# A two-layer decoder trunk on one core: first norm's squares summed per tile on TensorE, float32 logits in four column groups, moved constants, another block order

## The chip, the core and the metric

The kernel runs on one core of one Trainium2 chip. The metric is the device time of one execution in microseconds (us). The engines are TensorE (PE, matrix products, with a separate row PEld for weight loads), VectorE (DVE), ScalarE (ACT), GpSimd (POOL) and SyncE (SP), which here only issues DMAs. Each engine works through its own list of instructions in order.

## The reference, cut to what matters

512 tokens of 1024 float32 channels pass through two layers. The two places that the change touches directly are the first norm with the small logits made from it, and the logits of the forget gate after layer 0.

```python
def rms_norm(x, w):                       # mean over the 1024 channels of a token
    return x * rsqrt(mean(x * x, -1) + 1e-6) * w

# layer 0, mixer
h = rms_norm(x, pre_mix_norm[0])
proj = h @ w_in                           # 1024 x (8 heads x (k, q, v, z) x 128, and 16 columns)
b_logit, a_in = proj[..., o2:o2 + 8], proj[..., o2 + 8:]
beta = sigmoid(b_logit)
g = -exp(a_log) * softplus(a_in + dt_bias)
# q, k, v: convolution over 4 tokens and silu; then the gated delta rule per head, in chunks
...
# after layer 0
kvf = rms_norm(x, kv_norm) @ w_kv         # 1024 x (1024 keys, 1024 values, 16 columns)
f_logit = kvf[..., 2048:] + b_forget
log_f_cum = cumsum(log_sigmoid(f_logit))
# layer 1: attention with 16 heads of 64, its scores shifted by log_f_cum; each layer ends in a SwiGLU
```

## The kernel before, in words

**Tiles.** Everything lies transposed: a tile is 128 channels by 512 tokens, so the residual x is eight tiles (`a` in the profile). A product's weights come as blocks of 1024 rows by 128 columns, 512 KB each. A block (`wf`) is split into a high half `wh` (ScalarE's copy into float32r, the rounded type that TensorE multiplies in one pass) and a low half `wl` (block minus high half, on VectorE, sometimes GpSimd). x is split likewise after the norm's gain: pairs named `b` and `h`. `product` (L699) then makes three matmuls of 128x512 for each of the eight row tiles: high by high, low by high, high by low. A block is 24 such matmuls. Blocks are read in a fixed sequence (`seq`); `land` (L611) issues their loads on SP's queue, `halve` (L620) makes the halves, `next_halves` and `halver` (L658, L669) do so ahead of use. There are four buffers of each of wf, wh, wl.

**Order.** The program is written as cooperating generators that record instructions; `Plan.cost` (L202) gives each one an assumed time, `groups_of` (L302) joins neighbouring matmuls of one kind into groups of less than 0.8 us of that assumed time, and `listed` and `ordered` (L362, L412) sort the groups into one order per engine. So a change to any cost moves instructions everywhere. All instructions are issued from one helper and carry line 102 in the trace; they are told apart by their tiles. PSUM banks are `prj` (3 of them, for products), `mid` (2), `sm` (2) and `ob` (1).

**The start (`main`, L1592).** k0's weights come in four quarters of 128x256 between x's eight tiles, on SP's queue, and the small weights (1024x16, `w_small`) behind x's seventh tile and whole blocks behind all of it. The gains and four constants come on ScalarE's queue. TensorE first does 11 products of ones. Then, for each x tile, `halves_of` (L753) makes the pair (high half with the gain on ScalarE, low half on VectorE) and `accumulate` (L724) squares it on ScalarE and adds the square to one tile on VectorE. When all eight are added, `token_sums` (L730) sums over channels with 16 small matmuls (each 32 rows of output, one column), and `token_rsqrt` (L737) makes the factor `rs` per token: VectorE, a power on GpSimd, four transposes, a copy by ScalarE. Blocks that are multiplied before `rs` is there use the unscaled pairs and are multiplied by `rs` behind the product; `scaled_halves` (L1637) makes scaled pairs for the later ones. `first_factor` (L1633) runs the factor.

**Logits.** With k0 run the 16 columns of the small weights, its high and low halves side by side as 32 columns: `thin_product` (L706) makes two float32r matmuls of 32 rows of output for each x tile, 16 in all, into one bank `prj`. `gates` (L949) takes it from there: `token_logits` (L923) multiplies by `rs`, transposes four times 32 rows by 128 tokens into `sm`, and adds the halves. The same function serves the forget gate after layer 0 (`forget`, L1394), whose 16 matmuls stand in `main` at L1724 and read the second set of the norm `n2`.

**Blocks.** `GDN_ORDER` (L1557) lists the 32 blocks of k, q, z and v (8 heads each) in the order in which `main` multiplies them; the constants' casts (`identb` and others) and the recurrences of the heads stand among them.

Of the kernel before, what the change touches and what calls it, by code (L numbers as in the profile page):

```python
# [120 lines left out]
class Plan:  # L121
# [80 lines left out]
    def cost(self, eng, op, out, ins, kw):  # L202
# [8 lines left out]
        if eng == "PE":  # L211
# [224 lines left out]
def trunk(  # L436
# [183 lines left out]
    def halve(pieces=1, act=ACT, dve=None):  # L620
# [10 lines left out]
        elif not thin:  # L631
            lo = plan.tile("wl", 4, wpool, [P, KT, P], F32R, nm("wl"))
            ready.append((hi[:, :, :cols], lo[:, :, :cols]))
        else:

            lo = hi[:, :, cols:]
            ready.append(hi[:, :, : 2 * cols])
# [3 lines left out]
        step = n // pieces  # L641

# [94 lines left out]
    def token_rsqrt(acc, tok, r, use):  # L737
# [3 lines left out]
        yield ("#sm", plan.ready(acc[:, tok]))  # L741
        ps = sm()
        token_sums(ps, acc, cs)
# [15 lines left out]
    class Norm:  # L759


        def __init__(self, name, sets):
            self.name, self.sets = name, sets
            self.h = [[alloc() for _ in range(KT)] for _, alloc in sets]
            self.acc, self.rs, self.r = w_tile(), w_tile(), small([P, NC], "tokn", 2)

        def factor(self, i, tok):
# [3 lines left out]
            yield from token_rsqrt(self.acc, tok, self.r, use)  # L771
# [96 lines left out]
    def add(w, eng, n=KT, cols=P, thin=False, ahead=False):  # L868
# [54 lines left out]
    def token_logits(ps, norm, dst, n=2):  # L923
# [8 lines left out]
        part = ps[:, 0 : NC * m].rearrange("p (c i h) -> p c i h", i=n, h=16)  # L932
        DVE.tensor_copy(dst, part[:, :, 0])
        if n == 2:
            DVE.tensor_tensor(out=dst, in0=part[:, :, 1], in1=dst, op=ALU.add)
# [617 lines left out]
    def eng_mix():  # L1553
# [4 lines left out]
        "k0 k1 k2 z0 z1 k3 k4 k5 k6 q0 z2 k7 z3 z4 z5 z6 "  # L1558
        "z7 v0 q1 v1 q2 v2 q3 v3 q4 v4 q5 v5 q6 v6 q7 v7"
    ).split()]  # L1560
    for kind, hd in GDN_ORDER:
        add(w_gdn["qkvz".index(kind) * GH + hd], DVE)
        if (kind, hd) == ("k", 0):
            add(w_small[0], DVE, cols=16, thin=True)
# [17 lines left out]
    add(w_small[1], DVE, cols=16, thin=True)  # L1582
# [9 lines left out]
    def main():  # L1592
# [9 lines left out]
        ACT.dma_start(out=cst_sb, in_=cst[:, 0:2])  # L1602
# [212 lines left out]
```

## Time and profile before

| | |
|---|---|
| three runs | 1323.44, 1323.25, 1322.71 us |
| median | 1323.25 us |
| the profiled execution | 1322.56 us |
| its span in the trace | 1320.8 us |
| TensorE busy | 1307.2 us (99%) |
| VectorE, ScalarE, GpSimd busy | 768.5, 588.6, 105.7 us |

How to read it: the span is the time between the first and the last record of the profiled execution, the execution's own time is 1.8 us longer. Matmuls overlap in the pipeline, so the time of one (0.38 us in its record) is longer than the distance to the next. The page's chain of work that ended last is 98% TensorE. The rows on which the prediction rests follow below.

### The profile page before, as it was taken

Reading aid. Unit: us, or ns where it says so; the run is one execution under the profiler, and the core shown is the slowest. Engines: PE = TensorE matmul, PEld = TensorE weight load, DVE = VectorE, ACT = ScalarE, POOL = GpSimd, SP = SyncE. Lnnn points to the kernel's source line nnn. Section 1 sums busy time; section 2 is a strip of 40 time slices with the busy share of each in tenths; the row PEclk is TensorE's granted clock in tenths of the full one; section 3 lists DMA queues with packets and bytes.
Section 4 is the critical chain, followed back from the end, with each engine's and each line's share of the span. In section 5 each row is a group of like instructions: output and inputs, shape, how many; then the busy total and the mean of one; then the engine's idle time right before and its main releaser. Section 6 shows DMA issues by size and latency. Waiting matters only on the chain.

```text
span 1320.8 us, 19699 instructions
## 1 busy us (share of the span) xinstructions
PE 1307.2 (99%) x7906; PEld 1088.2 (82%) x7906; DVE 768.5 (58%) x1362; ACT 588.6 (45%) x1119; POOL 105.7 (8%) x104
## 2 busy tenths in 40 slices
PE   8999999999999999999999999999999999999997
PEld 6788788889988888888899787777988888888886
DVE  7979877757764432244468575787775444442223
ACT  6574466647432222233345474685543222223221
POOL 0020000003200000000022310200310000000000
PEclk8999999999999999999999999999999999999999
DMA  7213220215223233323321230201222222233121
GB/s 228 74 49 112 67 74 23 65 52 173 80 96 96 93 95 98 112 98 96 105 89 65 80 99 33 97 2 47 98 91 101 96 96 96 96 98 110 65 95 64
DMA packets 36683, 115.73 MB, mean 88 GB/s; under 512 B 6336, under 2 KB 7104, under 8 KB 36592
## 3 DMA queue, kind: packets, MB, share of 16 engines
q1 hardware_dynamic: 34720, 111.95, 25.8%
q10 hardware_dynamic: 1872, 2.53, 0.6%
q8 instruction: 62, 1.02, 0.3%
q14 instruction: 29, 0.24, 0.1%
HBM read 112.30 MB, written 2.16 MB: 87 GB/s over the span
## 4 chain that ended last, share of the span: by engine, by line
PE 98%; DMA 1%; issue 1%; DVE 0%; ACT 0%; ACTq 0%; DVEq 0%; POOLq 0%; POOL 0%
PE prj L102 78%; PE mid L102 7%; PE sm L102 6%; PE ob L102 6%; DMA wf<-in_w_gdn_dram 0%; DMA a<-in_xT_dram 0%; DVE w L102 0%; ACT w L102 0%; DVE b L102 0%; ACT b L102 0%; ACT y L102 0%; DVE h L102 0%; DVE a L102 0%; ACTq L102 0%; ACT wh L102 0%
## 5 line engine op out<-in xcount | busy, mean ns | idle before, releaser
L102 PE MATMUL prj<-h,wh 128*128 128x512 f32 (+1 forms) x1840 | 584.0, 388 | 0.0
L102 PEld LDWEIGHTS prj<-h,wh 128*128 128x128 f32 x1840 | 345.7, 188 | 66.1
L102 ACT ACTIVATE wh<-wf 128x1024 fp32r<-128x1024 f32 (+2 forms) x202 | 207.6, 1031 | 429.4 <-PE prj L102 212.4
L102 PE MATMUL prj<-h,wl 128*128 128x512 f32 (+1 forms) x920 | 353.3, 384 | 0.0
L102 DVE TENSOR_TENSOR wl<-wf,wh 128x1024 fp32r<-128x1024 f32 (+2 forms) x188 | 226.3, 1205 | 160.5 <-ACT wh L102 160.0
L102 PE MATMUL prj<-b,wh 128*128 128x512 f32 (+2 forms) x992 | 289.1, 369 | 3.7 <-ACT b L102 3.5
L102 PEld LDWEIGHTS prj<-b,wh 128*128 128x128 f32 (+1 forms) x992 | 176.0, 187 | 36.5 <-ACT b L102 4.9
L102 PEld LDWEIGHTS prj<-h,wl 128*128 128x128 f32 x920 | 173.2, 188 | 31.1
L102 DVE TENSOR_TENSOR w<-prj,w 128x512 f32<-128x512 f32 (+1 forms) x88 | 60.8, 691 | 202.4 <-PE prj L102 201.7
L102 PE MATMUL prj<-b,wl 128*128 128x512 f32 (+1 forms) x480 | 172.5, 359 | 0.0
L102 PEld LDWEIGHTS prj<-b,wl 128*128 128x128 f32 x480 | 91.3, 190 | 11.1
L102 DVE TENSOR_TENSOR w<-w,w 128x512 f32<-128x512 f32 (+1 forms) x123 | 81.4, 669 | 31.9 <-ACT w L102 27.0
L102 PE MATMUL prj<-wh,b 128*128 128x512 f32 x260 | 88.1, 399 | 0.0
L102 ACT ACTIVATE b<-w 64x512 fp32r<-64x512 f32 (+1 forms) x92 | 57.0, 628 | 24.5 <-DVE w L102 23.8
L102 PEld LDWEIGHTS prj<-wh,b 128*128 128x128 f32 x260 | 48.9, 188 | 10.2 <-issue 0.7
L102 PE MATMUL prj<-wl,b 128*128 128x512 f32 x130 | 50.7, 390 | 0.0
L102 PE MATMUL prj<-h,b 128*128 128x256 f32 x288 | 46.7, 284 | 0.0
L102 POOL TENSOR_TENSOR wl<-wf,wh 128x1024 fp32r<-128x1024 f32 x12 | 29.2, 2437 | 194.1 <-ACT wh L102 192.6
L102 DVE TENSOR_TENSOR b<-w,b 128x512 fp32r<-128x512 f32 (+1 forms) x60 | 42.3, 706 | 2.7 <-ACT b L102 2.3
L102 ACT ACTIVATE b<-sm,m 128x256 f32<-128x256 f32 (+3 forms) x64 | 33.4, 524 | 20.6 <-DVE m L102 20.3
L102 PEld LDWEIGHTS prj<-h,b 128*128 128x128 f32 x288 | 39.7, 192 | 0.0
L102 ACT ACTIVATE b<-prj 128x512 f32<-128x512 f32 (+1 forms) x49 | 26.5, 540 | 29.3 <-PE prj L102 29.3
(216 smaller groups left out, 1485.2 us busy)
## 6 DMA issues: line engine op xcount, KB each, us to landing
wf<-in_w_ffn_in_dram SPq DMA_DIRECT2D x88, 512.0 KB
wf<-in_w_gdn_dram SPq DMA_DIRECT2D x31, 512.0 KB
wf<-in_w_down_dram SPq DMA_DIRECT2D x22, 512.0 KB
wf<-in_w_ffn_out_dram SPq DMA_DIRECT2D x16, 512.0 KB
wf<-in_w_gdn_out_dram SPq DMA_DIRECT2D x8, 512.0 KB
wf<-in_w_q_dram SPq DMA_DIRECT2D x8, 512.0 KB
wf<-in_w_k_dram SPq DMA_DIRECT2D x8, 512.0 KB
wf<-in_w_v_dram SPq DMA_DIRECT2D x8, 512.0 KB
```

The source lines that it names most:

```text
L102: self.call(*[real(v) for v in self.args], **{k: real(v) for k, v in self.kw.items()})
```

## The change

- **Squares.** Each x tile's squares are summed by TensorE as they are made, into an `sm` bank held for it: eight sets of 16 small matmuls that accumulate. The additions on VectorE go; VectorE makes three of the squares (tiles 1, 3, 5), ScalarE five.
- **Loads.** k0's first quarter goes ahead of x's first tile; the four constants go from ScalarE's queue to SyncE's, behind x or among the weight blocks.
- **Scaled halves.** The low halves of the scaled pairs 1, 3 and 5 are made on GpSimd.
- **Block order.** `GDN_ORDER` is another permutation.
- **Logits.** `thin_product` makes one float32 matmul for each x tile from x itself and the small weights times the gain (on VectorE; 16 columns, 16 more set to zero by GpSimd): eight, each 32 rows of output, spread over four groups of output rows by k % 4. `token_logits` multiplies and transposes all 128 rows, and one reduction adds the four parts. The planner's cost of such a matmul is new, and `main` allows a switch to other work only after every fourth.

```diff
             elif cols == 32:
-                t = 0.021
+                t = 0.021 if n == 1 else n / 2400
...
+        def thin_weights():
+            w = f(hi)[:, :, :32]
+            POOL.memset(w[:, :, cols:], 0.0)
+            g = gains_sb[:, thin * KT : (thin + 1) * KT].unsqueeze(2).broadcast_to([P, KT, cols])
+            (dve or eng).tensor_tensor(out=w[:, :, :cols], in0=t[:, :, :cols], in1=g, op=ALU.mult)
...
-    def thin_product(ps, w, k, xp):
-        for i in range(2):
-            PE.matmul(ps[0:32], lhsT=w[:, k], rhs=xp[:, i], start=k == 0 and i == 0, stop=k == KT - 1 and i == 1)
+    def thin_product(ps, w, k, x):
+        PE.matmul(ps[ck(k % 4, 32)], lhsT=w[:, k], rhs=x[k], start=k < 4, stop=k >= 4)
...
-    def token_sums(ps, src, chunks):
+    def token_sums(ps, src, chunks, first=True, last=True):
...
-                          rhs=ones[:, 0:1], start=True, stop=True)
+                          rhs=ones[:, 0:1], start=first and (last or c == 0), stop=last and (first or c == NC - 1))
...
-        m = n * 16
-        DVE.tensor_tensor(out=rows[0:m], in0=ps[0:m], in1=norm.rs[0:m], op=ALU.mult)
+        DVE.tensor_tensor(out=rows, in0=ps, in1=norm.rs, op=ALU.mult)
...
-            PE.transpose(ps[:, ck(c, m)], rows[0:m, ck(c)], ident[0:m, 0:m])
...
+            PE.transpose(ps[:, ck(c)], rows[:, ck(c)], ident)
+        DVE.tensor_reduce(
+            out=dst, in_=ps.rearrange("p (c i h) -> p c h i", i=4, h=32)[:, :, 0:16], axis=AX.X, op=ALU.add)
...
-        "k0 k1 k2 z0 z1 k3 k4 k5 k6 q0 z2 k7 z3 z4 z5 z6 "
+        "k0 k1 z0 k2 k3 k4 k5 k6 z1 k7 q0 z2 z3 z4 z5 v0 "
...
-        ACT.dma_start(out=cst_sb, in_=cst[:, 0:2])
...
+        SP.dma_start(out=cst_sb, in_=cst[:, 0:2])
...
             if k > 1:
-                accumulate(n0.acc, x0[k - 2], k - 2, full, ACT, DVE)
+                sq = w_tile()
+                if k - 2 in (1,3,5):
+                    DVE.tensor_tensor(out=sq, in0=x0[k - 2], in1=x0[k - 2], op=ALU.mult)
+                else:
+                    ACT.activation(sq, x0[k - 2], AF.Square)
+                squares.append(sq)
...
+            for k in range(KT):
+                yield (plan.ready(squares[k]),)
+                token_sums(sums, squares[k], range(NC), k == 0, k == KT - 1)
...
-                    DVE.tensor_tensor(out=hs[k - 1][:, 1], in0=t[k - 1], in1=f(hs[k - 1][:, 0]), op=ALU.subtract)
+                    (POOL if k - 1 in (1, 3, 5) else DVE).tensor_tensor(
+                        out=hs[k - 1][:, 1], in0=t[k - 1], in1=f(hs[k - 1][:, 0]), op=ALU.subtract)
...
-                    thin_product(pb, ws[1], k, h[k])
+                    thin_product(pb, ws[1], k, x0)
...
         for k in range(KT):
-            thin_product(ps, w, k, n2.h[1][k])
-            yield ()
+            thin_product(ps, w, k, x)
+            if k % 4 == 3:
+                yield ()
```

TensorE's order at the start, before, from the product with x's fourth tile on. `prj_152` is k0's bank, `prj_193` the logits' bank, `b_` the pairs of x, `sm_214` the sums, `mid_251` the transposed factor.

```order
L102 MATMUL prj_152<-b_183,wh_131 128x512
L102 MATMUL prj_152<-b_183,wl_140 128x512
L102 MATMUL prj_152<-b_183,wh_131 128x512
L102 MATMUL sm_214<-ones,w_117 32x1 x16
L102 MATMUL prj_193<-b_183,wh_181 32x512 x2
L102 MATMUL prj_193<-b_189,wh_181 32x512 x2
L102 MATMUL prj_193<-b_200,wh_181 32x512 x2
L102 MATMUL prj_193<-b_205,wh_181 32x512 x2
L102 MATMUL mid_251<-cst_sb,tokn_244 128x128 x4
L102 MATMUL prj_193<-b_211,wh_181 32x512 x2
```

One set of sums stood there, and five pairs of logit matmuls in a near row. The same place after, with `prj_137` as k0's bank, `prj_185` the logits', `a_` x itself, `sm_157` the sums:

```order
L102 MATMUL prj_185<-a_97,wh_114 32x512
L102 MATMUL prj_185<-a_104,wh_114 32x512
L102 MATMUL prj_185<-a_110,wh_114 32x512
L102 MATMUL sm_157<-ones,w_182 32x1 x16
L102 MATMUL prj_137<-b_175,wh_119 128x512
L102 MATMUL prj_137<-b_175,wl_123 128x512
L102 MATMUL prj_137<-b_175,wh_119 128x512
L102 MATMUL sm_157<-ones,w_213 32x1 x16
L102 MATMUL prj_185<-a_117,wh_114 32x512
L102 MATMUL prj_137<-b_189,wh_119 128x512
L102 MATMUL prj_137<-b_189,wl_123 128x512
L102 MATMUL prj_137<-b_189,wh_119 128x512
```

Three logit matmuls stand in a row, and from the fourth on each stands alone between k0's matmuls or the sums. SyncE's queue of DMAs at the start, before:

```order
L102 DMA a_83<-in_xT_dram 128x512
L102 DMA a_97<-in_xT_dram 128x512
L102 DMA a_104<-in_xT_dram 128x512
L102 DMA wf_109<-in_w_gdn_dram 128x256
L102 DMA a_113<-in_xT_dram 128x512
L102 DMA a_119<-in_xT_dram 128x512
L102 DMA wf_109<-in_w_gdn_dram 128x256
L102 DMA a_124<-in_xT_dram 128x512
L102 DMA a_129<-in_xT_dram 128x512
L102 DMA wf_134<-in_w_small_dram 128x8x16
```

Seven x tiles and two of k0's quarters stood ahead of the small weights. After:

```order
L102 DMA wf_87<-in_w_gdn_dram 128x256
L102 DMA a_97<-in_xT_dram 128x512
L102 DMA a_104<-in_xT_dram 128x512
L102 DMA wf_87<-in_w_gdn_dram 128x256
L102 DMA a_110<-in_xT_dram 128x512
L102 DMA wf_87<-in_w_gdn_dram 128x256
L102 DMA a_117<-in_xT_dram 128x512
L102 DMA wf_121<-in_w_small_dram 128x8x16
L102 DMA wf_87<-in_w_gdn_dram 128x256
L102 DMA a_128<-in_xT_dram 128x512
L102 DMA a_133<-in_xT_dram 128x512
L102 DMA a_141<-in_xT_dram 128x512
```

Four x tiles and three quarters stand ahead of the small weights, and a quarter stands first. TensorE's order at the forget gate's logits, before, with the last matmul of the block ahead of them:

```order
L102 MATMUL prj_6944<-h_6566,wh_6826 128x512
L102 MATMUL prj_6991<-b_6424,wh_6854 32x512 x2
L102 MATMUL prj_6991<-b_6474,wh_6854 32x512 x2
L102 MATMUL prj_6991<-b_6485,wh_6854 32x512 x2
L102 MATMUL prj_6991<-b_6516,wh_6854 32x512 x2
```

and after, where x's tiles (`a_`) are read:

```order
L102 MATMUL prj_7043<-h_6665,wh_6925 128x512
L102 MATMUL prj_7090<-a_3521,wh_6953 32x512
L102 MATMUL prj_7090<-a_3528,wh_6953 32x512
L102 MATMUL prj_7090<-a_3535,wh_6953 32x512
L102 MATMUL prj_7090<-a_3541,wh_6953 32x512
L102 MATMUL prj_7090<-a_3546,wh_6953 32x512
```

Sixteen matmuls became eight, in a row in both orders, of which the fences show the first.

## Rows read from the trace of the kernel before

**Rows 1.** The page: span, TensorE's busy time, instructions
```profile
span 1320.8 us, 19699 instructions
...
PE 1307.2 (99%) x7906; PEld 1088.2 (82%) x7906; DVE 768.5 (58%) x1362; ACT 588.6 (45%) x1119; POOL 105.7 (8%) x104
```

**Rows 2.** Stretches of 2 us: length, busy time (instructions) by engine, clock, DMA, GB/s
```profile
6.00:8.00 2.00, 0.00 (x0) 0.00 (x0) 0.72 (x2) 1.38 (x3) 0.00 (x0) 1.00 1.04 386
8.00:10.00 2.00, 1.60 (x3) 0.72 (x3) 1.90 (x4) 2.00 (x6) 0.00 (x0) 0.59 1.02 256
10.00:12.00 2.00, 1.22 (x2) 0.50 (x2) 2.00 (x5) 2.00 (x6) 0.00 (x0) 0.50 0.95 269
...
14.00:16.00 2.00, 2.00 (x8) 0.94 (x7) 2.00 (x4) 2.00 (x5) 0.00 (x0) 0.70 0.95 334
```

**Rows 3.** Order of time on TensorE, 8 to 24 us: start, time, instruction, tiles, count
```profile
8.22 0.67 PE L102 MATMUL prj<-b,wh 128*128 128x512 f32 x1 [2.59 <-ACT b L102]
...
16.36 0.40 PE L102 MATMUL prj<-b,wh 128*128 128x512 f32 x1
16.68 0.43 PE L102 MATMUL sm<-ones,w 128*32 128x1 f32 x32
17.05 2.03 PE L102 MATMUL prj<-b,wh 128*32 128x512 f32 x8
...
21.37 0.43 PE L102 MATMUL sm<-cst_sb,w 32*128 32x32 f32 x4
21.73 0.50 PE L102 MATMUL prj<-b,wh 128*128 128x512 f32 x1
...
23.00 0.62 PE L102 MATMUL prj<-b,wh 128*128 128x512 f32 x2
...
23.68 0.62 PE L102 MATMUL prj<-b,wh 128*128 128x512 f32 x2
```

**Rows 4.** Order of time, all engines, 0 to 14 us: first x, small weights, halves
```profile
3.75 1.39 ACT L102 ACTIVATE w<-a 128x512 f32<-128x512 f32 x2 [1.52 <-DMA a<-in_xT_dram]
...
6.98 0.64 SPq L102 DMA_DIRECT2D wf<-in_w_small_dram  x1
7.15 0.40 ACT L102 ACTIVATE wh<-wf 128x256 fp32r<-128x256 f32 x1
...
7.46 0.71 ACT L102 ACTIVATE b<-a,gains_sb 128x512 fp32r<-128x512 f32 x1
...
11.68 0.29 ACT L102 ACTIVATE wh<-wf 128x128 fp32r<-128x128 f32 x1
```

**Rows 5.** Order of time on TensorE in attention: matmuls of 64 output rows
```profile
781.60 1.09 PE L102 MATMUL ob<-b,h 128*64 128x128 f32 x16
...
791.95 0.88 PE L102 MATMUL ob<-b,h 128*64 128x128 f32 x12
```

**Rows 6.** Order of time on TensorE: the second norm's logits
```profile
735.60 4.11 PE L102 MATMUL prj<-b,wh 128*32 128x512 f32 x17
739.54 0.40 PE L102 MATMUL prj<-b,wl 128*128 128x512 f32 x1
```

**Rows 7.** Later stretches, columns as in rows 2
```profile
20.00:60.00 40.00, 40.00 (x181) 31.46 (x180) 37.74 (x69) 21.42 (x36) 0.00 (x0) 1.00 0.37 119
...
340.00:680.00 340.00, 340.00 (x1602) 284.00 (x1601) 150.08 (x186) 106.64 (x143) 6.51 (x4) 1.00 0.32 103
```

**Rows 8.** Order of time on TensorE at the end of the recurrences
```profile
289.00 0.49 PE L102 MATMUL sm<-rhs,b 128*128 128x128 f32 x2 [0.64 <-DVE rhs L102]
```

**Rows 9.** GpSimd's weight halves as a group, then the order of time near 703
```profile
L102 POOL TENSOR_TENSOR wl<-wf,wh 128x1024 fp32r<-128x1024 f32 x12 | 29.2, 2437 | 194.1 <-ACT wh L102 192.6 <-issue 1.5
...
702.81 1.76 DVE L102 SCALAR_TENSOR_TENSOR h<-a,gains_sb,h 128x256 fp32r<-128x256 f32 x2
703.37 0.92 POOL L102 TENSOR_TENSOR a<-b,a 128x256 f32<-128x256 f32 x1
...
705.23 0.47 DVE L102 SCALAR_TENSOR_TENSOR h<-a,gains_sb,h 128x256 fp32r<-128x256 f32 x1
```

More of the change, by code (lines that the diff above doesn't have):

```diff
@@ L630, in halve @@
             ready.append((hi, lo))
-        elif not thin:
+        elif thin is None:
             lo = plan.tile("wl", 4, wpool, [P, KT, P], F32R, nm("wl"))
@@ L641, in halve @@
         step = n // pieces
+        def thin_weights():
[3 more added lines that the diff above has]
+            (dve or eng).tensor_tensor(out=w[:, :, :cols], in0=t[:, :, :cols], in1=g, op=ALU.mult)
+        if thin is not None:
+            return [thin_weights]
         def piece(k):
@@ L734, in token_sums, with token_rsqrt @@
                 PE.matmul(ps[ck(b, 32), c : c + 1], lhsT=src[:, c * P + b * 32 : c * P + b * 32 + 32],
-                          rhs=ones[:, 0:1], start=True, stop=True)
-    def token_rsqrt(acc, tok, r, use):
+                          rhs=ones[:, 0:1], start=first and (last or c == 0), stop=last and (first or c == NC - 1))
+    def token_rsqrt(acc, tok, r, use, ps=None):
         cs = range(tok.start // P, tok.stop // P)
         sl = slice(cs[0], cs[-1] + 1)
-        yield ("#sm", plan.ready(acc[:, tok]))
-        ps = sm()
-        token_sums(ps, acc, cs)
+        if ps is None:
+            yield ("#sm", plan.ready(acc[:, tok]))
+            ps = sm()
+            token_sums(ps, acc, cs)
+        else:
+            yield (plan.ready(ps[:, sl]),)
         m = small([P, NC], "tokr", 4)
@@ L759, in trunk, with __init__ @@
     class Norm:
-        def __init__(self, name, sets):
+        def __init__(self, name, sets, sums=None):
             self.name, self.sets = name, sets
             self.h = [[alloc() for _ in range(KT)] for _, alloc in sets]
-            self.acc, self.rs, self.r = w_tile(), w_tile(), small([P, NC], "tokn", 2)
+            self.sums = sums
+            self.acc, self.rs, self.r = None if sums is not None else w_tile(), w_tile(), small([P, NC], "tokn", 2)
         def factor(self, i, tok):
@@ L769, in use @@
                 ACT.activation(self.rs[:, tok], ps, AF.Copy)
-            yield from token_rsqrt(self.acc, tok, self.r, use)
+            yield from token_rsqrt(self.acc, tok, self.r, use, self.sums)
             signal(f"{self.name}.rs{i}")
@@ L866, in trunk, with add @@
     AHEAD = 3
-    def add(w, eng, n=KT, cols=P, thin=False, ahead=False):
+    def add(w, eng, n=KT, cols=P, thin=None, ahead=False):
         seq.append((w, n, eng, cols, thin, ahead))
@@ L921, in softplus_parts, with token_logits @@
         dve.scalar_tensor_tensor(out=dst, in0=e, scalar=2.0, in1=relu, op0=ALU.mult, op1=ALU.add)
-    def token_logits(ps, norm, dst, n=2):
+    def token_logits(ps, norm, dst):
         rows = w_tile()
-        m = n * 16
-        DVE.tensor_tensor(out=rows[0:m], in0=ps[0:m], in1=norm.rs[0:m], op=ALU.mult)
+        DVE.tensor_tensor(out=rows, in0=ps, in1=norm.rs, op=ALU.mult)
         yield ("done", "#sm")
@@ L1601, in main @@
             go()
-        ACT.dma_start(out=cst_sb, in_=cst[:, 0:2])
-        ACT.dma_start(out=cst_w[:, 0 : 3 * P].rearrange("p (a b) -> p a b", b=P), in_=cst[:, 2:5])
-        ACT.dma_start(out=heads_sb, in_=heads)
-        ACT.dma_start(out=conv_sb, in_=conv)
+        SP.dma_start(out=cst_sb, in_=cst[:, 0:2])
+        SP.dma_start(out=cst_w[:, 0 : 3 * P].rearrange("p (a b) -> p a b", b=P), in_=cst[:, 2:5])
+        SP.dma_start(out=heads_sb, in_=heads)
+        SP.dma_start(out=conv_sb, in_=conv)
         DVE.memset(ones, 1.0)
@@ L1614, in main @@
         plan.drop(warm)
-        n0 = Norm("n0", [(PRE_MIX, b_pair)])
+        sums = sm()
+        plan.hold(sums)
+        n0 = Norm("n0", [(PRE_MIX, b_pair)], sums)
         hs = [h_pair() for _ in range(KT)]
@@ L1618, in main @@
         first, logits = halve(4, ACT, DVE), halve(1, ACT, DVE)
+        squares = []
         for k in range(KT + 2):
@@ L1633, in first_factor @@
         def first_factor():
+            for k in range(KT):
+                yield (plan.ready(squares[k]),)
+                token_sums(sums, squares[k], range(NC), k == 0, k == KT - 1)
+            plan.hold(sums, False)
             yield from n0.factor(0, full)
```

14 lines of the change are left out of this document (5 added, 9 removed).

## The prediction, made before the changed kernel ran

> **What bounds the kernel now.** I read the page first: TensorE (PE) is busy for 1307.2 of 1320.8 us [rows 1]. A busy PE is not a fast one, so the table by stretches comes next: from 20 us on no stretch shows PE idle and the clock is full, and in 340 to 680 us 1602 matmuls fill 340 us without a gap [rows 7]. There a change pays only if it takes work off PE. The first 20 us are different: PE is idle from 6 to 8 us, and between 8 and 16 us it runs at half clock with gaps [rows 2]. The order of time on PE shows what this costs: the first matmul on data starts at 8.22, and the logits' transposes stand at 21.37; six matmuls of block k0 follow from 21.73, so that k1, the second block, begins at about 23.2 [rows 3]. Up to there PE has 24 matmuls of k0 at 0.227 us (23.00 to 23.68 is 0.68 for three [rows 3]), 16 of the logits at 0.23 (17 matmuls of the same kind and its neighbour take 3.94 from 735.60 to 739.54 [rows 6]), the sums and some transposes, 10.5 us in all. So 4.5 us behind 8.22 are waits and half clock. The engines that feed it there are ScalarE and VectorE, both busy for 2.00 of 2.00 us from 10 to 12 us [rows 2].
>
> The sum is made against the profiled execution (1322.56 us: a span of 1320.8 and 1.8 around it), and 0.7 us is then added, since the median of the runs is 1323.25. Measurement can tell about 0.2% (2.65 us) from no change.
>
> **The start, from 0 to k1.** x's first tile was usable at 3.75 us [rows 4]. Now k0's first quarter of weights and the gains are ahead of it or beside it, half its size, and ScalarE has no squares to make first: the weights' high half (0.40 us) and x's (0.71) follow at once [rows 4], and PE can begin at about 5.0 instead of 8.22. It does not keep this gain. The new logits need wh, made on VectorE from the 64 KB of small weights. Before, these were issued at 6.98 behind 2.5 MB and were read at 11.68 [rows 4]; now 1.5 MB are ahead. One MB at the 256 to 386 GB/s of 6 to 10 us [rows 2] is 3 us, so they land near 8.5. VectorE waits for them in its order, with a square and x3's low half queued behind, and multiplies in about 0.29 (ScalarE's row of the same size, [rows 4]); PE's first logit matmul starts at about 9.2. The nine matmuls of k0 and one set of sums ahead of it need 2.5 us and are done by then.
>
> What one step costs. **Sums:** a set of 32 instructions stands between 16.68 and 17.05, and the matmul ahead of it at 16.36, so it adds 17.05 - 16.36 - 0.227 = 0.46: 0.26 of work, 0.10 for each change of operand kind [rows 3]. **Float32 logits:** none is in the trace with 512 columns. The nearest rows are matmuls of 64 rows of output and 128 columns, two passes to each, that alternate between two column groups: 16 instructions take 1.09 us and 12 take 0.88, so one pair more costs 0.21 [rows 5], and one of 512 columns four times that, 0.85. I take it that four groups run beside each other as two do; a matmul alone still takes 0.85. The old 512-column form took 0.231 [rows 6].
>
> The new order gives a triple, then five single ones, each between matmuls of another kind; the order fence ahead shows it. From the first logit matmul on, PE has: triple and sums 0.85 + 0.26 + 0.20 = 1.31; x3 0.68; sums and a single 1.31; x4 0.68; a single and five sums 0.85 + 1.30 + 0.20 = 2.35; x5 0.68; a single 1.05; x6 0.68; a single 1.05; x7 0.68; a single and four transposes (0.44) 1.49. Together 12.0, and 0.3 for a wait on ScalarE's square of x2. So k1 begins at 9.2 + 12.3 = 21.5 instead of 23.2: **-1.7 us**. The gain of 3.2 at the front and most of the 4.5 of waits is spent on 7 more sets of sums (+2.4 with the kinds' changes) and on singles (6.0 with theirs against 3.7).
>
> What this covers. VectorE has eight low halves, four of weights, three squares: some 10 us from 4.6 on, with waits done by about 17, and PE wants x7's low half near 19. The identity lands behind k1's weights, near 15, and VectorE's cast of it stands ahead of x6's low half: if it came after 17, every us would go onto PE. The seven additions of squares that fall away on VectorE and three squares on ScalarE are worth nothing beyond this, since PE is then the late one. The issues of four constants leave ScalarE's queue and stand in SyncE's, 0.3 to 0.65 each, behind x or k1's weights; behind them wait z0's and k2's weights, which PE wants after 26 us. Low halves on GpSimd and the memset are hidden likewise (price below).
>
> A rule of the Trainium skill speaks against these singles. The row: old 32-wide matmuls follow 128-wide ones with no gap beyond 0.23 [rows 6], and only the sums show 0.10 at a change [rows 3]. TensorEngine Tiling (Array Packing), Key Properties, says that a change of tiling mode drains TensorE. By a full drain, 0.39 - 0.23 = 0.16 at each of 14 changes, k1 would begin 0.8 us later.
>
> **Logits of the second norm.** Sixteen matmuls from 735.60 to 739.3 took 3.7 us on PE, one behind the other [rows 6]. Now eight stand in a row, two rounds of four groups: 2 x 0.85 + 0.20 = 1.9. **-1.8 us.** Ends: -2.9 with no cost of change and passes that overlap further, +3.1 with no overlap at all (8 x 0.85).
>
> **Small terms.** Four transposes of 128 rows instead of 32, twice: 0.44 for 0.36, **+0.2**. In the attention stage the new order changes kind some eight times more, at 0.05 to 0.1: **+0.4**. The block order only swaps z blocks against k blocks: PE has the same 5.4 us for each, and the wait left at its end, 0.64 [rows 8], stands in the same four-matmul pattern in the new order: 0, with 1 us either way.
>
> Sum: -1.7 - 1.8 + 0.2 + 0.4 = -2.9; 1322.56 - 2.9 + 0.7 = **1320.4 us**, the likeliest.
>
> **Rivals.**
> (a) The clock falls. It fell at 8 us because PE stood idle from 6 to 8, and was half until about 15 [rows 2]. Now PE works from 5 on, with gaps of about 1 us while it waits for squares and wh. If they are enough, up to 5.8 us behind 9.2 are at half clock, worth 1 to 2.9 us: 1321.4 to 1323.3, middle 1322.4. For: the gaps. Against: most of the time is filled.
> (b) Only two groups overlap, as the 64-wide row shows two [rows 5]. Second logits 8 x 0.85 / 2 + 0.2 = 3.6 (saves 0.1), the triple +0.85: 1322.9. The Trainium skill's page TensorE: Matmul & The Clock Gate, Measured speedup, gives 2.38 for three column tiles of 512; an estimate by it is 2.1 for the eight, in between.
> (c) Singles are cheaper: they run beside a neighbour or the waits hide them. Five fall from 0.85 to 0.23: -3.1, 1317.3. Nothing in the rows shows a neighbour of another kind overlapping.
> (d) Slower: VectorE falls behind. It is busy for 37.7 of 40 us from 20 to 60 [rows 7]. GpSimd now takes three halves of 512 (1.2 each, half of 2437 ns) and one weight half of 2.44 us, and while GpSimd worked for 0.92 two VectorE instructions took 1.76, where one alone takes 0.47 [rows 9]: 6.1 us x 0.88 = 5.4 us longer on VectorE, and one block more is multiplied by rs there (0.68). It is relieved of 3.3. If none of it is hidden, the weights' low halves queued behind are late and PE waits up to 6.1: 1326.5. It decides once VectorE is over 5.5 us late, when 1325.9 is passed. Against: the list puts the weights' halves blocks ahead, and relief and 2.3 us idle cover most.
> That GpSimd's part does nothing is inside the forecast.
>
> **How the numbers follow.** Forecast 0.53 (own range 1318.9 to 1321.9; 0.35 of it below 1320.6, the line of 0.2%, and 0.18 above, since its middle is just beyond the line), (a) 0.13, (b) 0.12, (c) 0.12, (d) 0.10. Faster by over 0.2%: 0.35 + 0.12 = 0.47; within: 0.18 + 0.13 + 0.12 = 0.43; slower: 0.10. The range, 1317.0 to 1324.0, takes in (a), (b) and (c) with 0.3 to 0.7 us on their far side, and leaves out (d) and the tails of the forecast.
>
> **What would show it.** In the new profile: first matmul on data near 5 us; first logit matmul near 9; a lone one followed after 0.85 to 0.95, and 0.23 would be (c); granted clock from 8 to 16 us at 1.00, and 0.50 is (a); k1's first matmul at 21.5; the eight second logits in 1.9 us, and 3.5 is (b); PE without idle time in 20 to 60, and waits on wl there are (d). I am wrong if small weights land much after 9, or if a stretch behind 25 us moves by over 1.5 us.

## The result, and the profile after

The changed kernel takes 1329.65 us (median of four runs, 1329.31 to 1332.29) against 1322.98 for the kernel before: a ratio of the means of 1.0055 with a 95% interval from 1.0043 to 1.0066. The forecast was 1320.4 with a range of 1317.0 to 1324.0, so it was wrong, in sign and in size. The profiled execution has a span of 1327.5 us, 6.7 above before.

The page's first lines of the changed kernel answer to [rows 1]:

```profile
span 1327.5 us, 20144 instructions
...
PE 1312.6 (99%) x8130; PEld 1091.5 (82%) x8130; DVE 772.6 (58%) x1352; ACT 587.0 (44%) x1114; POOL 114.9 (9%) x111
```

Still 99%, so the page doesn't show where the time went. Stretches do (length, busy time and instructions by engine, granted clock, DMA share, GB/s), here of the changed kernel:

```profile
180.00:190.00 10.00, 10.00 (x65) 8.85 (x64) 5.86 (x19) 5.54 (x20) 1.26 (x2) 1.00 0.14 52
190.00:196.00 6.00, 3.24 (x102) 2.43 (x100) 5.42 (x9) 4.91 (x12) 0.00 (x0) 0.92 0.28 90
196.00:202.00 6.00, 5.73 (x31) 4.95 (x32) 3.12 (x11) 2.74 (x6) 1.01 (x1) 0.51 0.00 0
```

and the same stretches of before:

```profile
180.00:190.00 10.00, 10.00 (x141) 7.87 (x140) 7.27 (x16) 6.37 (x17) 1.19 (x2) 1.00 0.17 54
190.00:196.00 6.00, 6.00 (x53) 4.89 (x48) 3.98 (x12) 3.76 (x9) 1.01 (x1) 1.00 0.00 0
196.00:202.00 6.00, 6.00 (x69) 5.21 (x68) 5.59 (x14) 3.53 (x11) 0.00 (x0) 1.00 0.28 91
```

In the stage of the recurrences TensorE now stands idle for 2.8 of 6 us, in pieces of at most 0.81 us, and for the next 6 us the granted clock is 0.51, the lower of its two levels (1.2 GHz). I call this the hole. Its price is 3.0 us of idle time up to 197 and 6 x 0.49 + 6 x 0.08 = 3.4 us of clock; 0.8 us of the idle time lies where the clock is already low, so 0.4 is counted twice, and the hole costs 6.0. The view of TensorE's waits, 186 to 300 us, says for what it waited:

```profile
PE mid L102 <- ACT a L102: 1.6, 3, 0.8
PE ob L102 <- ACT y L102: 1.1, 2, 0.7
PE mid L102 <- DVE w L102: 0.8, 1, 0.8
PE sm L102 <- DVE rhs L102: 0.6, 1, 0.6
```

The last line and 0.46 of the second stand at the end of the recurrences, where before has the same two waits (0.64 [rows 8] and 0.46). The rest is the hole. TensorE's order of time, its first two and its last three lines there:

```profile
189.29 0.40 PE L102 MATMUL prj<-h,wh 128*128 128x512 f32 x1
189.53 0.60 PE L102 MATMUL mid<-cst_sb,w 128*128 128x128 f32 x4
...
196.27 1.48 PE L102 MATMUL mid<-b,w 64*64 64x64 f32 x16 [0.81 <-DVE w L102]
197.68 0.90 PE L102 MATMUL mid<-cst_sb,b 128*128 128x128 f32 x3
198.23 0.78 PE L102 MATMUL prj<-h,wh 128*128 128x512 f32 x1
```

What waits are steps of `merge` (blocks of the inverse for heads 2 and 3) and of a recurrence, which wait for each other's copies; no 128x512 matmul stands between them in TensorE's list from 189.5 to 198.2.

Milestones give the whole account. Differences to before, from matmuls that both kernels have: k1 begins at 23.06 instead of 23.23 (-0.2); the last matmul of the recurrences is at 296.1 instead of 290.2, so 6.1 were lost between; the second logits begin at 741.61 instead of 735.60 (+0.1 more), and take 1.9 us less; the attention's last output matmul is at 922.2 instead of 915.5 (+2.6 on the way); the rest to the end of the span changes little (-0.1). Sum: -0.2 + 6.1 + 0.1 - 1.9 + 2.6 - 0.1 = 6.6, against 6.7; the 0.1 is rounding.

### The profile page after: what moved, and what is told of

Read it like the earlier page. It is cut to its first block, busy times and chain, and to the rows that moved or that the text cites. A ratio compares the mean times of both kernels' runs of the same rounds, so it can differ in the third digit from the quotient of the medians.

```text
span 1327.5 us, 20144 instructions
## 1 busy us (share of the span) xinstructions
PE 1312.6 (99%) x8130; PEld 1091.5 (82%) x8130; DVE 772.6 (58%) x1352; ACT 587.0 (44%) x1114; POOL 114.9 (9%) x111
## 3 DMA queue, kind: packets, MB, share of 16 engines
q8 instruction: 64, 1.05, 0.3%
## 4 chain that ended last, share of the span: by engine, by line
PE 97%; DVE 1%; ACT 1%; issue 0%; DMA 0%; SPq 0%; ACTq 0%; DVEq 0%; POOLq 0%; POOL 0%
PE prj L102 78%; PE mid L102 7%; PE sm L102 6%; PE ob L102 6%; DVE b L102 0%; DMA a<-in_xT_dram 0%; DVE w L102 0%; ACT w L102 0%; ACT b L102 0%; DVE m L102 0%; ACT wh L102 0%; SPq L102 0%; DVE h L102 0%; DVE a L102 0%; ACT a L102 0%
## 5 line engine op out<-in xcount | busy, mean ns | idle before, releaser
L102 ACT ACTIVATE wh<-wf 128x1024 fp32r<-128x1024 f32 (+1 forms) x200 | 207.6, 1039 | 444.6 <-PE prj L102 214.1
L102 DVE TENSOR_TENSOR wl<-wf,wh 128x1024 fp32r<-128x1024 f32 (+2 forms) x186 | 223.7, 1204 | 168.3 <-ACT wh L102 164.4
L102 PE MATMUL prj<-b,wh 128*128 128x512 f32 (+1 forms) x976 | 286.0, 367 | 0.1
L102 PEld LDWEIGHTS prj<-b,wh 128*128 128x128 f32 x976 | 175.3, 190 | 31.5 <-issue 4.7
L102 DVE TENSOR_TENSOR w<-prj,w 128x512 f32<-128x512 f32 x88 | 60.8, 691 | 198.1 <-PE prj L102 194.5
L102 PE MATMUL prj<-b,wl 128*128 128x512 f32 (+1 forms) x488 | 175.2, 359 | 0.0
L102 DVE TENSOR_TENSOR w<-w,w 128x256 f32<-128x256 f32 (+1 forms) x116 | 74.4, 649 | 26.5 <-ACT w L102 21.3
L102 POOL TENSOR_TENSOR wl<-wf,wh 128x1024 fp32r<-128x1024 f32 x14 | 34.6, 2474 | 204.7 <-ACT wh L102 162.8
L102 DVE TENSOR_REDUCE m<-sm 128x1 f32<-128x256 f32 (+3 forms) x64 | 30.4, 485 | 13.4 <-PE sm L102 13.0
```

Of the source, the lines that this page charges most:

```text
L102: self.call(*[real(v) for v in self.args], **{k: real(v) for k, v in self.kw.items()})
```

## The experiments

Two words for what follows. The **31 steps** are the loop in `inverse` in which VectorE inverts the diagonal blocks, two instructions of up to 0.43 us to a step. A time given for the last of them is the start of its multiplication. The **first recurrence** is the first matmul `ob<-y,b`. Both depend on the chain rs, gates, decays, k blocks, steps, `merge`.

### Undoing one part at a time

**e1_old_order**, the table of blocks put back in the changed kernel:

```diff
-        "k0 k1 z0 k2 k3 k4 k5 k6 z1 k7 q0 z2 z3 z4 z5 v0 "
+        "k0 k1 k2 z0 z1 k3 k4 k5 k6 q0 z2 k7 z3 z4 z5 z6 "
...
```

> The changed kernel with the block order of before (the GDN_ORDER table alone is put back). Theory A, the block order: in the changed kernel VectorE's 31 steps of the inverse end at 155.7 us instead of 148.7, the first head's recurrence begins at 173.2 instead of 165.9, and TensorE runs out of blocks at 190, stands idle for 3 us and then runs 6 us at half clock; with the old table the steps end near 149, no idle time of over 1 us is left between 180 and 200, and the time is 1323 to 1324.5, about 6 under the changed kernel. Theory B, GpSimd's low halves: the hole is there with any table, and the time stays at 1328 to 1330.

Measured: 1333.21 us, ratio to before 1.0080 (1.0064 to 1.0095): slower still, and outside what either theory gave. The last step is at 162.6, not 149.

**e2_dve_halves**:

```diff
-                    (POOL if k - 1 in (1, 3, 5) else DVE).tensor_tensor(
+                    DVE.tensor_tensor(
```

> The changed kernel with the three scaled low halves back on VectorE. Theory B: while GpSimd works between 34 and 46 us, VectorE's small instructions on sp take 0.40 and 0.74 us instead of 0.18 and 0.17, the gates are 4 us late, and the inverse behind them too; without it the steps end near 152 and the time is 1324 to 1326. Theory A: VectorE gets 2.0 us of halves back and the small instructions are fast again; the 31 steps still end at 154 to 157, the hole stays, and the time is 1328 to 1331.

Measured: 1335.47 us, 1.0095 (1.0080 to 1.0110), again outside both. The gates do get shorter, as theory B says: from the first instruction on `sp` to the last on `g` they take 17.6 us (31.7 to 49.3), as in before, where the changed kernel takes 23.2 (28.7 to 51.9). That helps neither the steps nor the time, since the start was listed anew too: k1 begins at 27.7, behind a standstill of TensorE that e4 shows more closely, and the last step is at 160.1.

**e3_order_only**, the kernel before with the new table:

```diff
-        "k0 k1 k2 z0 z1 k3 k4 k5 k6 q0 z2 k7 z3 z4 z5 z6 "
+        "k0 k1 z0 k2 k3 k4 k5 k6 z1 k7 q0 z2 z3 z4 z5 v0 "
...
```

> The kernel before with the new block order alone. Theory A: the 31 steps end 4 to 7 us later than 148.7, TensorE has a hole between 180 and 200, and the time is 1327 to 1330, 4 to 7 over before. Theory B: 1322 to 1324, no hole.

Measured: 1330.05 us, 1.0054 (1.0039 to 1.0069), with a hole at 184 to 196. So in the total the table alone costs what the whole change costs; but e1 shows that the rest without the table costs more. Nor do the two add up: from k1 to the last matmul of the recurrences the table alone loses 9.8 us against before (20.0 to 296.7), the rest alone 9.9 (e1, 23.0 to 299.9), both together 6.1.

**e4_thin_last**:

```diff
                     product(ps, ws[0], k, h[k], k == 0, k == KT - 1)
-                    thin_product(pb, ws[1], k, x0)
                     yield (plan.ready(h[min(k + 1, KT - 1)][:, 1]),)
+                for k in range(KT):
+                    thin_product(pb, ws[1], k, x0)
+                    if k % 4 == 3:
+                        yield ()
```

> The changed kernel with the first norm's eight logits written behind k0's products instead of one after each, so that they stand as 3, 4 and 1 in TensorE's order. A lone logit matmul costs 1.08 us there (17.94 to 18.92 and 0.1 ahead of it), eight in a row cost 1.85 after layer 0. Theory A and the price of lone ones: k1 begins at 20.5 to 21.5 instead of 23.06. Whether the end gains the same 2 us depends on what sets the hole at 190: 1327.5 if the 31 steps on VectorE come earlier too, 1329.5 if VectorE, which has the same work, still sets it.

Measured: 1331.25 us, 1.0059 (1.0042 to 1.0076), above both values expected. The start got worse, k1 at 25.7. VectorE's order of time shows the hazard that the prediction had named for the changed kernel, where it didn't strike, and TensorE's what happened beside it:

```profile
17.43 0.23 DVE L102 CAST identb<-cst_sb 128x128 bf16<-128x128 f32 x1 [2.95 <-DMA cst_sb<-in_cst_dram]
...
17.71 0.74 DVE L102 SCALAR_TENSOR_TENSOR b<-a,gains_sb,b 128x512 fp32r<-128x512 f32 x1
```

```profile
13.38 0.88 PE L102 MATMUL sm<-ones,w 128*32 128x1 f32 x84
17.36 0.81 PE L102 MATMUL sm<-ones,w 128*32 128x1 f32 x44 [3.10 <-issue]
```

The cast of the identity waits 2.95 us for its DMA, and the low half of an x tile behind it in the list waits with it. But TensorE, which stands for 3.1 us and then works at half clock to 24, goes on at 17.36, ahead of both. It stands in the middle of the sums, whose squares were all made by 14.1, and "issue" means that it waits for nothing that the profile shows. What falls into these 3.1 us is a transfer of a queue that the profile calls `instruction`, 16 KB from 14.84 on. The same stands in e2 (transfer at 14.47, 2.9 us until 16.80) and in e9 below (13.92, 4.0 us until 16.40), and with 0.2 us in the changed kernel (13.61, until 16.27); before has its first such transfer at 20.08 and no such wait. So TensorE seems to stand until its own instructions have come, of which eight sets of sums use up more than one; that is read from the times, and no run tests it.

What the four have in common stands in this table. The last column but one gives idle time and lost clock ((1 - granted clock) x length) between 180 and 210; up to 0.5 us of idle time at low clock stands in both.

| kernel | last of the 31 steps | first recurrence | blocks begun by then | idle + clock lost | time |
|---|---|---|---|---|---|
| before | 148.7 | 165.9 | 23 | 0 + 0 | 1322.98 |
| changed | 155.7 | 173.2 | 24 | 3.0 + 3.4 | 1329.65 |
| e1_old_order | 162.6 | 180.3 | 25 | 3.2 + 3.4 | 1333.21 |
| e2_dve_halves | 160.1 | 179.4 | 24 | 2.4 + 5.1 | 1335.47 |
| e3_order_only | 152.0 | 174.0 | 24 | 4.1 + 3.4 | 1330.05 |
| e4_thin_last | 156.9 | 174.6 | 24 | 1.9 + 3.4 | 1331.25 |

Blocks are counted at 24 matmuls each. In each of the five kernels with a hole 25 blocks have begun ahead of it, and the 26th is what ends it, at 198.2 in the changed kernel. The times show what it comes behind. q3 is the 23rd block; its product is made early, but the convolution that takes it out of its PSUM bank runs only after head 0's recurrence (the blocks q3 to v7 are recorded when the state of an earlier head is done, `yield (f"s{hd - 3}",)` in `main`, for heads from 3 on; which buffer holds the convolution back wasn't traced). ScalarE's first part of it, in the changed kernel and in before:

```profile
192.78 0.68 ACT L102 ACTIVATE b<-prj,conv_sb 128x512 f32<-128x512 f32 x1
```

```profile
185.73 0.67 ACT L102 ACTIVATE b<-prj,conv_sb 128x512 f32<-128x512 f32 x1
```

Until then blocks 23, 24 and 25 fill the three banks `prj`, so, by the code and these times, 25 blocks are all that TensorE has. In the five kernels the 26th begins 5.1 to 6.2 us behind that convolution's start, and 21 to 27 us behind the first recurrence. A kernel in which the recurrences begin late has spent its 25 blocks too early, and nothing is left to stand between the recurrences' waits. In before the 25th block ends at 193.6, when the convolution is done, and no gap opens.

### Is it VectorE's work on the chain?

A small edit keeps every list as it is and only issues an instruction not at all, or twice:

```diff
             for item in group.items:
-                item.issue()
+                for _ in range(getattr(item, "times", 1)):
+                    item.issue()
```

**e5_steps_left_out**: the changed kernel, `times = 0` for both instructions of steps 11 to 18, so it leaves out part of the inverse.

> The changed kernel with every engine's order kept, in which 8 of the 31 steps of the inverse (16 instructions of 0.42 us on VectorE, no work of TensorE) are left out: it makes no right inverse. Theory A2: the chain from the gates over the 31 steps to the first recurrence sets when TensorE has work to put between its blocks; it is 7 us late in the changed kernel (first recurrence 173.2 instead of 165.9), and the hole at 190 and the half clock behind it are its price. Then the first recurrence moves to about 166.5, the hole and the half clock are gone, and the time is 1322.5 to 1324.5. Theory C: the holes come from how the new order happens to be laid out on TensorE, whatever the chain does; then the time is 1328 to 1330.

Measured: 1329.06 us, 1.0048 (1.0034 to 1.0061), as theory C says. Nothing was won: the first recurrence is at 173.5, and the hole is there. VectorE's groups in 114 to 156 us, first in the changed kernel, then in this one, show where the time went (instructions, busy time, mean, idle before and its cause):

```profile
L102 DVE TENSOR_TENSOR pr<-b,b 128x31 f32<-128x31 f32 (+15 forms) x31 | 10.5, 340 | 0.7
...
L102 DVE TENSOR_TENSOR wl<-wf,wh 128x1024 fp32r<-128x1024 f32 x8 | 9.8, 1219 | 2.5 <-ACT wh L102 2.4
...
L102 DVE SCALAR_TENSOR_TENSOR b<-prj,conv_sb,b 128x511 f32<-128x511 f32 (+2 forms) x5 | 3.7, 746 | 1.3 <-ACT b L102 1.3
```

```profile
L102 DVE TENSOR_TENSOR wl<-wf,wh 128x1024 fp32r<-128x1024 f32 x8 | 9.8, 1221 | 4.8 <-ACT wh L102 4.7
L102 DVE TENSOR_TENSOR pr<-b,b 128x31 f32<-128x31 f32 (+11 forms) x23 | 7.2, 314 | 0.5
...
L102 DVE SCALAR_TENSOR_TENSOR b<-prj,conv_sb,b 128x511 f32<-128x511 f32 (+2 forms) x4 | 3.0, 749 | 4.5 <-ACT b L102 4.4
```

The steps are listed among low halves of weights and convolutions of later blocks. Those wait for ScalarE, which waits for TensorE's blocks. With fewer steps VectorE waits longer there, 4.8 and 4.5 us instead of 2.5 and 1.3, and the last step is at 155.9, where the changed kernel has 155.7. Theory A2 is refuted in its simple form: not the work on the chain sets the time, but its place in the list, between which blocks each step stands.

**e8_before_left_out**, the same on the kernel before:

> Control: the kernel before, order kept, with the same 8 of 31 steps left out (no right inverse). Theory A2: before has no hole, so its TensorE is full and the shorter chain gives nothing, 1322.3 to 1323.3. If it gains 3 us or more, the chain sets the end there too, and the comparison of the changed kernel needs that amount taken off.

Measured: 1322.86 us, 0.9999 (0.9990 to 1.0009). No gain, as for a full TensorE.

**e7_before_longer**: before, `times = 2` for the multiplication of steps 7 to 22.

> The kernel before with every engine's order kept, in which 16 of the 31 steps do their multiplication twice: 16 instructions of 0.40 us more on VectorE, 6.3 us in all, on the chain of the inverse. Theory A2: the first recurrence moves from 165.9 to about 172, a hole of some us opens near 185 to 200 with a fall to half clock behind it, and the time is 1327 to 1331. Theory C: TensorE's list has room for it, and the time stays within 1322.5 to 1324.5.

Measured: 1328.65 us, 1.0043 (1.0029 to 1.0056). The price is as expected, the place isn't. TensorE's order of time and two stretches of it:

```profile
143.80 0.60 PE L102 MATMUL mid<-cst_sb,a 128*128 128x128 f32 x4
148.00 1.22 PE L102 MATMUL mid<-b,b 128*128 128x128 f32 x4 [3.60 <-ACT b L102]
```

```profile
144.00:147.00 3.00, 0.40 (x4) 0.16 (x2) 2.96 (x9) 0.67 (x1) 0.00 (x0) 1.00 0.53 173
147.00:153.00 6.00, 5.00 (x16) 4.33 (x17) 3.56 (x10) 2.62 (x7) 0.00 (x0) 0.52 0.29 92
```

VectorE's delay of 6.3 us runs into TensorE's list at the next place where it waits for a tile `b` of ScalarE, 3.6 us idle, and the clock nearly doubles the price: 3.4 us more, of which 0.4 is counted twice. In this execution k1 came 0.6 earlier than in before, and the time is 5.6 us longer. More work on VectorE costs, less gains nothing: the list has no slack one way, and fixed places the other. The first recurrence is at 171.9 here, nearly as late as in the changed kernel, but still with 23 blocks begun, and no idle time stands between 180 and 210. So it is the number of blocks listed ahead of it that counts, and not how late it is.

### Another draw of the list

**e12_q5_first**: the changed kernel, one exchange in the table.

```diff
-        "z6 q1 z7 v1 q2 v2 q3 v3 q4 v4 q5 v5 q6 v6 q7 v7"
+        "z6 q1 z7 v1 q2 v2 q3 v3 q4 q5 v4 v5 q6 v6 q7 v7"
```

> The changed kernel with one pair of blocks exchanged: q5, which waits for no recurrence that isn't done, ahead of v4. Theory C2: v4 waits for an earlier head's recurrence and TensorE has nothing else in its list at 190; with q5 there the hole at 190 and the half clock behind it are gone, and the time is 1322.5 to 1324. But the exchange draws the whole list anew: if the block that fills the hole at 190 is missing earlier, a new hole opens there, and the time stays at 1327 to 1331. By theory A2 the hole stays at 185 to 200.

Measured: 1325.80 us, 1.0023 (1.0014 to 1.0032), so 3.9 us faster than the changed kernel, between the two ranges expected. The hole is gone, and from k1 to the last matmul of the recurrences 1.0 us is lost against before instead of 6.1; the attention takes 1.2 us more than in the changed kernel:

```profile
180.00:190.00 10.00, 10.00 (x139) 7.91 (x138) 8.10 (x18) 7.22 (x19) 0.23 (x1) 1.00 0.18 55
190.00:202.00 12.00, 12.00 (x117) 10.17 (x116) 10.24 (x26) 7.34 (x19) 1.92 (x1) 1.00 0.14 45
```

The reason that I gave was wrong: q5 does wait for a recurrence, for that of head 2, a later one than v4's. What the exchange did is draw the whole list anew, far ahead of its own place as well: the steps begin at 109.6 instead of 113.95, though the gates are as late as in the changed kernel (the last on `g` ends at 52.0); the last step is at 148.4, the first recurrence at 164.4, and only 22 blocks have begun by then. Whether the pair's exchange at its own place also helps is left open; the runs don't separate it from the earlier start of the recurrences.

**e9_no_hole**: a draw of the changed kernel whose list has no place of this kind, with another price of a first logit matmul in the planner, larger groups, another table and GpSimd for the casts of the constants.

```diff
-                t = 0.021 if n == 1 else n / 2400
+                t = 0.021 if n == 1 else 0.215
...
-        if same and it.outs[0].tensor is g.items[-1].outs[0].tensor and g.busy + it.busy < 0.8:
+        if same and it.outs[0].tensor is g.items[-1].outs[0].tensor and g.busy + it.busy < 0.9:
...
+        "k0 k1 z0 k2 k3 k4 k5 z1 k6 q0 k7 z2 z3 z4 z5 z6 "
+        "z7 v0 q1 v1 q2 v2 q3 v3 q4 q5 v4 v5 q6 v6 q7 v7"
...
-        DVE.tensor_copy(identb, ident)
+        POOL.tensor_copy(identb, ident)
...
```

(with the other three casts, e2's and e4's edits).

> The changed kernel with another draw of its order: the eight first logits behind k0's products in two fours (the planner's price of one 0.215 us and its groups up to 0.9 us, so that fours stay together), the four casts of constants on GpSimd, so that VectorE doesn't wait for their DMA, the scaled low halves on VectorE, and a block order with q5 ahead of v4, so that a block that waits for no recurrence is there when v4 waits. Theory C2: what the change lost is the hole at 190 and the half clock behind it, because TensorE's list has no block there that may run; a list without such a hole keeps what the change gains (second logits -2.0, first logits in a row). Then no idle time of over 1 us between 30 and 285, full clock, first recurrence anywhere, and 1313 to 1318. Theory A2, the chain of the 31 steps as such sets the end: the chain is no shorter here, so a hole stays and it is 1322 to 1330.

Measured: 1319.66 us, 0.9975 (0.9966 to 0.9984): faster than both kernels, though short of the 1318 that I had put as its upper end, and in neither range expected. First recurrence at 164.6 with 22 blocks begun, and a full TensorE from 180 to 285 at full clock. It still loses 4 us of idle time at 12.4 to 16.4, in the middle of a set of sums and with "issue" as the cause, like e4, and k1 begins at 25.2. So many parts differ from the changed kernel here that the run shows what a list without a hole takes, and not which part is to be thanked.

**e11_slower_dma**: as e9, with another table of blocks and

```diff
-            return size / 380e3, 3.0 if eng == "SP" else 3.3 + size / 60e3
+            return size / 300e3, 3.0 if eng == "SP" else 3.3 + size / 60e3
```

> Like e9_no_hole, with the planner's price of a transfer at 300 instead of 380 GB/s (the rows of the first 16 us show 245 to 379) and a block order drawn for that, again with q5 ahead of v4. In e9_no_hole the sums of squares were listed ahead of x's last tiles on TensorE and waited for them from 12.4 to 16.4 us, and the clock was half from 14 to 21. With the later landing in the plan the sums stand among k0's products: no wait of over 1.5 us before 20, k1 begins at 21 to 23 instead of 25.2, and, if no hole opens later, the time is 1314.5 to 1318. If the list opens a hole elsewhere, 1318 to 1324.

Measured: 1321.15 us, 0.9987 (0.9978 to 0.9996). The start was mended in part: the standstill is down to 0.4 us and k1 at 23.2, a little beyond the 21 to 23 expected, with the granted clock at 0.50 from 9.8 to 20. The recurrences end at 287.5, 1.4 earlier than in e9; but the attention came out worse (last output matmul at 914.9 instead of 912.4). It has waits of 1.2 us at 776 and 1.4 at 876 that e9 hasn't, and 3.4 us at half clock behind the second. The profile is of one execution of 1322.70, above the median, so how much of this the others have is open. The gain at the start was given back 500 us and more later, by the same kind of redraw.

### The attention, and GpSimd beside VectorE

**e6_second_only**: before, with the forget gate's logits alone in float32 (`thin_product`, `token_logits` and the loop at L1724 as in the change, for the second norm only).

> The kernel before with the forget gate's logits alone made in float32 in four column groups; the order of all engines is that of before up to them. Logits 1.85 us instead of 3.95: -2.0 us there; four wider transposes +0.1; by theory A2 nothing else moves ahead of 735 us, and 1321.0 is expected. By theory D, that any new order in the attention stage costs 1 to 3 us (782.75 and 907 us show 1.4 and 0.8 of new waits in the changed kernel), it is 1322 to 1324.

Measured: 1323.84 us, 1.0006 (0.9997 to 1.0015), in the range of theory D. Up to the logits it is before, to 0.1 us. There, in TensorE's order of time:

```profile
735.69 1.92 PE L102 MATMUL prj<-a,wh 128*32 128x512 f32 x16
737.55 0.50 PE L102 MATMUL prj<-b,wh 128*128 128x512 f32 x1
```

1.86 us, where [rows 6] had 16 matmuls in 3.7. And then 2.6 us are lost again on the way to the attention's last output matmul. One piece of it, all engines, weight loads left out:

```profile
775.22 2.98 DVE L102 TENSOR_SCALAR b<-b,m 128x512 f32<-128x512 f32 x2
...
775.33 2.59 POOL L102 TENSOR_TENSOR wl<-wf,wh 128x1024 fp32r<-128x1024 f32 x1 [7.07 <-DVE m L102]
...
778.26 0.66 PE L102 MATMUL mid<-cst_sb,b 128*128 128x128 f32 x4 [1.18 <-DVE b L102]
```

**e10_half_on_act** takes GpSimd out of it; the low half of one block of weights is zeros:

```diff
+                        nc.scalar.activation(o, i0, AF.Copy, scale=0.0)
+                        continue
                 item.issue()
```

> The kernel with the second logits alone (e6_second_only), order kept, in which one low half of a weight block, GpSimd's 2.59 us at 775.3, isn't computed: ScalarE writes zeros in its place (1.06 us, in a place where it stood idle for 0.8). Theory E: beside GpSimd's subtraction VectorE's two multiplications by a factor took 2.98 us instead of 0.87, and TensorE waited 1.18 us for the second; without it they take 0.9, the wait at 777 is gone, and the time falls by 0.8 to 1.2 us, to 1322.6 to 1323.1. Theory F: the two took so long for another reason (a queue, the buffer they read), and nothing changes: 1323.5 to 1324.2.

Measured: 1322.96 us, 0.9999 (0.9991 to 1.0008), 0.9 below e6. The two intervals overlap, but the traces agree: from the logits to the attention's last output matmul it takes 1.15 us less. The two multiplications are quick and the wait is gone:

```profile
775.41 0.87 DVE L102 TENSOR_SCALAR b<-b,m 128x512 f32<-128x512 f32 x2
```

Theory E holds: 2.98 us beside GpSimd, 0.87 without. The Trainium skill's page SBUF — State Buffer, section Who interferes with whom, says that VectorE in a two-port mode and GpSimd block each other fully. The trace fits: of the two multiplications the first takes 0.48 us, and the second 2.59 and ends 0.28 behind GpSimd's instruction; in which mode they ran no run shows. The changed kernel has the same wait at 784, and a further one of 0.6 us for ScalarE at 908; the remaining 0.9 of its 2.6 are spread and weren't traced to a cause.

## Why the prediction was wrong, step by step

**The step that failed** is in the small terms: "The block order only swaps z blocks against k blocks ... 0, with 1 us either way". I read the new order where before had its waits [rows 8], found the same pattern, and put no price on the rest. The stretch from k1 to the recurrences' end, which the sum leaves as it was, lost 6.1 us, at a place where before has no wait at all; the hole there is 6.0 of it. It isn't the table's work that costs: put back alone (e1) it makes the loss larger. Each edit, to the table or to a cost, gives the planner another list, and it is the list that has the hole or not. Why this list puts the steps and the recurrences later wasn't traced into the planner. A second step sits under it: rival (d) asked whether VectorE would have too much work, not whether the steps of the inverse would stand later in its list. Its price, 6.1 us, is the measured one by luck. The first half of its mechanism shows: beside GpSimd three of the gates' small instructions take 1.87, 1.28 and 1.29 us, where others like them take 0.18. The second half, late weights for which TensorE waits in 20 to 60, doesn't (40.00 of 40 us busy), and e2, which takes GpSimd's halves away, doesn't mend the time.

**The start.** Forecast -1.7, measured -0.2. Three terms were short, each by rows of the changed kernel:

```profile
5.27 0.85 PE L102 MATMUL mid<-ones 128*128 128x128 f32 x3
...
5.77 0.77 PE L102 MATMUL prj<-b,wh 128*128 128x512 f32 x1
```

```profile
10.10 0.63 PE L102 MATMUL prj<-a,wh 128*32 128x512 f32 x3
...
17.61 0.40 PE L102 MATMUL prj<-b,wh 128*128 128x512 f32 x1
17.94 1.04 PE L102 MATMUL prj<-a,wh 128*32 128x512 f32 x2
18.92 0.50 PE L102 MATMUL prj<-b,wh 128*128 128x512 f32 x1
19.25 0.39 PE L102 MATMUL prj<-b,wl 128*128 128x512 f32 x1
...
22.65 0.65 PE L102 MATMUL mid<-cst_sb,tokn 128*128 128x128 f32 x4
```

TensorE begins on data at 5.77, when the products of ones are through, not at 5.0. The first logit matmul is at 10.10 instead of 9.2: VectorE had the small weights ready at 9.5, but a wait of 0.63 for a square ahead of it moved all. And a lone logit matmul costs 0.98, 0.10 ahead of it and 0.10 in the first matmul behind it (0.33 where others take 0.23), 1.18 where the sum had 1.05; the piece with five sums took 2.67 (14.38 to 17.05) instead of 2.35. So the way from the first logit to k1 is 12.96, where the sum had 12.0 and 0.3 for a wait that now fell ahead of it. (The 2.5 MB that the prediction puts ahead of the small weights in before are 2.3 by the sizes of the transfers; the landing came out about right all the same.) The clock, rival (a), stayed at 1.00 from 8 to 20 us. There is a cost that I didn't see at all: the factor rs is ready on GpSimd in both kernels at the same time (17.4 and 1.5 us more), but its transposes stand on TensorE behind the lone logits, at 22.65 instead of 18.95. The gates begin 6 us later. In e1, with the old table, the steps begin 6 us later as well (117.1 instead of 110.8), in the changed kernel 3 (113.95), and in e12, with gates as late, 1.2 earlier: so late gates alone don't make late steps. From the first step to the last, the changed kernel takes 41.7 us, before 37.9, e1 45.5.

**The second logits** were right: -1.8 forecast, -1.9 measured. One alone takes 0.98 and eight in a row 1.85: 8 x 0.98 / 1.85 = 4.2, so four column groups run side by side (above four, since a lone one bears the change of kind behind it by itself), and rivals (b) and (c) fall. The Trainium skill's page TensorE: Matmul & The Clock Gate, Measured speedup, has 2.38 for three groups of 512 columns; in proportion that would be 3.2 for four, an estimate from the page. These rows show more, and the measurement decides.

**The attention** was put at +0.4 for changes of kind. It is +2.6, of which e6 and e10 explain 1.15 by GpSimd beside VectorE.

**The change of kind** on TensorE: 0.10 ahead of a lone float32 matmul, 0.10 in the first matmul behind it, and 0.98 - 0.85 = 0.13 between, if 0.85, an estimate of the forecast, is its own time. That is 0.33 for the two changes around it, where the sum had 0.20 and a full drain at each would have been 0.32. So the drain, which the forecast set aside, fits these rows better than its own 0.10.

## What to carry to other kernels

Where a scheduler draws each engine's order from a table of costs, an edit is two things: its own work, which rows can price, and a new draw of everything, ahead of it and behind it, which they can't. Ten draws of this kernel (before, changed, e1 to e4, e6, e9, e11, e12) lie between 1319.7 and 1335.5 us; measure an edit with the order kept as well as redrawn before saying that it is good or bad. Look in the new order for places where the bounding engine's list has only links of one chain and no independent work, count what is left to stand between them (here the blocks that the free PSUM banks allow), and price a hole there at about twice its idle time where the clock falls behind it (6.0 for 3.0 us in the changed kernel, 6.6 for 3.6 in e7).

## What the runs showed of the hardware

- Idle pieces of at most 0.81 us, together 2.8 of 6 us, are followed by 6 us at a granted clock of 0.51 (190 to 202 in the changed kernel); one idle time of 3.6 us in e7 has the same price, 3.4 us of clock.
- Eight float32 matmuls with 32 rows of output and 512 columns, over four column groups, take 1.85 us; one alone takes 0.98.
- VectorE's 128x512 multiplication by a factor takes 0.87 us for two, and 2.98 beside a GpSimd subtraction of 2.59. Instructions of 0.18 us on 128x32 take 1.28 to 1.87 beside GpSimd.
- In the first 20 us TensorE stands for 2.9, 3.1 and 4.0 us (e2, e4, e9) in the middle of a run of small matmuls, with no cause that the profile shows but a 16 KB transfer of the `instruction` queue in it.
